# A RetNet block with its MLP: the second norm by halves of rows with its pieces further apart, one pair of operands tile by tile, and weight sums one POOL operation at a time

## The chip, the cores and the metric

The kernel runs on 1 core of one Trainium2 chip. A time is the device time of one execution in microseconds (us). The span of a profile runs from the first to the last instruction of the core. Three runs of the kernel before gave 1489.48, 1494.76 and 1496.14 us, so its time is the median, 1494.76 us. The profiled execution took 1489.55 us, and its span is 1487.8 us.

## What is computed

The depth is 1 and the mixer is retention, so the reference comes down to this (1024 tokens, 1024 features, 4 heads, an MLP of 4096):

```python
h = rmsnorm(x, norm_mix_pre)
q, k, v, g = split(h @ ret_w_in)            # 1024, 1024, 2048, 2048 columns
o = causal retention per head (decay gamma_h, head size 256 / 512)
o = head_norm(o, ret_gn) * silu(g)
x = x + rmsnorm(o @ ret_w_out, norm_mix_post)
h = rmsnorm(x, norm_mlp_pre)
h = square(relu(h @ mlp_w_up)) @ mlp_w_down
out = x + rmsnorm(h, norm_mlp_post)
```

## The kernel before

Every matmul with full precision is three: an operand is split into a high part (ACT copies it to fp32r) and a low part (DVE subtracts the copy from the source), and high x high, high x low and low x high are added up in PSUM. The gate, out, up and down matmuls are done in blocks of two by two with seven products in place of eight (`SEVEN`, L479), so sums of blocks are needed on both sides.

Work is laid down as a list of *units* in the order of TensorE's work. A unit's cost is its count of 512-column matmuls. Everything else hangs on that list: a `Job` names how many units of cost ahead of its use a load or a split is issued, a `background` entry (L516, L537) names a place in the first stage, and a piece of a norm stands in a `Chunks` list with a place of its own. An engine then runs its instructions strictly in the order in which they were laid down; SP issues all DMAs, also in order.

The stages are: (1) projections and retention by head, up to about 495 us, with the background: `weight_sums` loads 1 MB of w_out or w_down, POOL forms four sums of blocks (L509) and SP stores them, 24 times through one buffer (`sums_pool`); `feature_sums` does the same for the normed rows, 4 times, with four rebuilds (L526) and four sums (L531). Head norms (L407) and the causal masks (`affine_select`, L367, on POOL) run among them. (2) The gates, to about 665 us. (3) `down_stage("r")`, the out projection, L852: seven products m = 0 to 6 of 96 matmuls each, in steps of 24 whose operands are loaded 64 and split 34 units ahead (`Step`, L799; two staging buffers, three operand tiles in `acts3`). The last product is the one where the last `O_OUTER` = 2 steps are done together, output tile by output tile. (4) `Up`: `fill` (L686) runs the first two products of all 16 column pairs, 384 matmuls, with TensorE accumulating the second product into the bank that ACT has just copied to `k_u` (L641). It needs only rows 4 to 7 of the normed activations; the other five products (`rest`) need rows 0 to 3 too. (5) `down_stage("m")`, and the last norm, `fin`.

The second norm, `mix`, ties (3) to (4). It handles two rows of tiles at a time (u = 0, 1: rows 4 to 7; u = 2, 3: rows 0 to 3):
- `mix_a` (L979): ACT squares both rows of 1024 and takes the root; POOL multiplies both rows by the gain, four operations of 512 (L942).
- `mix_b` (L984): DVE makes 1/root with five small operations (`inverse`, L947), adds the row to the residual (L945); SP stores it; ACT squares the result.
- `mix_c` (L991): DVE again `inverse`, then the normed row (L994).
- `mix_first` (u < 2): TensorE transposes (L1004), ACT and DVE split. `mix_d`, `mix_e`, `mix_f` (u >= 2): transposes, then four sums of blocks, each split by ACT and DVE. `mix_f` ends with two DVE operations (L1052, L1053), the ACT copy of T4 (L1054) and its low part.

Places are counted from the start of product m = 5 (0); m = 6 ends at 192. Up to 192 a piece is laid down after the next 6 units; from then on `between` (L1113) calls `mix.place` only after every 24: at 216, 240, 264 and so on to 576. Of these stops 216, 264, 312, ... come after two first products (whose `k_u` copies stand just before), and 240, 288, 336, ... after two second ones. In the kernel before, `mix_a` of rows 0 and 1 has place 196, `mix_b` 218, `mix_c` 244, `mix_d` 262 and 302, `mix_e` 276 and 316, `mix_f` 288 and 328; rows 2 and 3 come 150 later.

## Time and profile before

| | before |
|---|---|
| median of 3 runs | 1494.76 us (1489.48 to 1496.14) |
| the profiled execution | 1489.55 us |
| its span | 1487.8 us |
| TensorE busy in it | 1435.7 us (96%) |
| VectorE (DVE), ScalarE (ACT), GpSimd (POOL) busy | 870.1, 567.4, 401.2 us |
| mean granted TensorE clock | 0.988 |

A page of the profile gives each engine's busy time. The view of waits names for one engine which instruction waited for which. The timeline lists instructions in order of time, merged; at the end of a line, in brackets, is the idle time before it and what ended it. The view of windows gives for a stretch of time the busy time of each engine and the clock that TensorE was granted (1.00 is 2.4 GHz, 0.50 is 1.2 GHz; a figure between them is a mean over the stretch).

### The profile page before, as it was taken

Reading aid. Unit: us, or ns where it says so; the run is one execution under the profiler, and the core shown is the slowest. Engines: PE = TensorE matmul, PEld = TensorE weight load, DVE = VectorE, ACT = ScalarE, POOL = GpSimd, SP = SyncE. Lnnn points to the kernel's source line nnn. Section 1 sums busy time; section 2 is a strip of 40 time slices with the busy share of each in tenths; the row PEclk is TensorE's granted clock in tenths of the full one; section 3 lists DMA queues with packets and bytes.
Section 4 is the critical chain, followed back from the end, with each engine's and each line's share of the span. In section 5 each row is a group of like instructions: output and inputs, shape, how many; then the busy total and the mean of one; then the engine's idle time right before and its main releaser. Section 6 shows DMA issues by size and latency. Waiting matters only on the chain.

```text
span 1487.8 us, 17555 instructions
## 1 busy us (share of the span) xinstructions
PE 1435.7 (96%) x6417; PEld 1179.5 (79%) x6417; DVE 870.1 (58%) x1194; ACT 567.4 (38%) x857; POOL 401.2 (27%) x344
## 2 busy tenths in 40 slices
PE   8999999999999999999998798999999999999996
PEld 6887888878888788788886676888888788888875
DVE  6446146356335468874448677588778553445556
ACT  6322222213222442234445455354454444343442
POOL 1213546254633003431002231234443300000212
PEclk9999999999999999999999999999999999999998
DMA  6316556455534697777565545576677755455654
GB/s 245 124 73 211 198 169 221 151 192 207 222 115 157 208 322 230 251 258 234 206 245 212 179 157 184 184 248 221 221 244 237 244 220 187 174 212 214 232 218 169
DMA packets 177623, 304.76 MB, mean 205 GB/s; under 512 B 11761, under 2 KB 85505, under 8 KB 177026
## 3 DMA queue, kind: packets, MB, share of 16 engines
q1 hardware_dynamic: 177394, 303.39, 58.9%
q8 instruction: 50, 0.82, 0.2%
q14 instruction: 35, 0.29, 0.1%
q10 hardware_dynamic: 144, 0.26, 0.0%
HBM read 207.14 MB, written 96.47 MB: 204 GB/s over the span
## 4 chain that ended last, share of the span: by engine, by line
PE 79%; DVE 7%; DMA 4%; issue 4%; ACT 4%; POOL 1%; SPq 0%; DVEq 0%; ACTq 0%; POOLq 0%
PE pXm L848 12%; PE pqk L299 12%; PE pv L324 11%; PE pXr L848 6%; PE pZu L565 5%; PE pVu L565 5%; PE pVg L565 3%; PE pYm L848 3%; PE pZg L565 3%; PE pYu L565 3%; PE pXu L565 2%; PE po L378 2%; DMA st_m<-in_mlp_w_down_dram 2%; PE pst L399 2%; PE pXg L565 2%
## 5 line engine op out<-in xcount | busy, mean ns | idle before, releaser
L841 DVE TENSOR_TENSOR o_m<-st_m,o_m 128x1024 fp32r<-128x1024 f32 (+1 forms) x84 | 135.3, 1639 | 143.1 <-ACT o_m L837 141.9
L509 POOL TENSOR_TENSOR wsum<-wsum 128x512 f32<-128x512 f32 x96 | 127.5, 1328 | 159.8 <-DMA wsum<-in_ret_w_out_dram 73.6
L837 ACT CAST o_m<-st_m 128x1024 fp32r<-128x1024 f32 (+1 forms) x84 | 110.6, 1338 | 134.9 <-DMA st_m<-wdt_T 51.9
L848 PE MATMUL pXm<-o_m 128*128 128x512 f32 x480 | 115.2, 394 | 4.0 <-DVE o_m L841 3.3
L848 PE MATMUL pXm<-o_m,o_m 128*128 128x512 f32 x480 | 113.0, 390 | 0.9 <-DVE o_m L841 0.9
L848 PE MATMUL pXr<-o_r 128*128 128x512 f32 x480 | 110.3, 390 | 1.7 <-DVE o_r L841 1.7
L848 PEld LDWEIGHTS pXm<-o_m 128*128 128x128 f32 x480 | 91.0, 190 | 24.6 <-DVE o_m L841 4.5
L848 PEld LDWEIGHTS pXr<-o_r 128*128 128x128 f32 x480 | 89.8, 188 | 20.6 <-DVE o_r L841 2.1
L848 PEld LDWEIGHTS pXm<-o_m,o_m 128*128 128x128 f32 x480 | 90.0, 188 | 20.1 <-DVE o_m L841 1.5
L841 DVE TENSOR_TENSOR o_r<-st_r,o_r 128x2048 fp32r<-128x2048 f32 x28 | 65.4, 2339 | 63.2 <-ACT o_r L837 63.0
L942 POOL TENSOR_TENSOR yd<-yd,gain 128x512 f32<-128x512 f32 x15 | 23.5, 1592 | 281.4 <-ACT junk L180 281.4
L324 PE MATMUL pv<-wv_0h,hT 128*128 128x512 f32 x256 | 86.7, 400 | 0.0
L324 PE MATMUL pv<-wv_1h,hT 128*128 128x512 f32 x256 | 86.0, 395 | 0.0
L1107 ACT ACTIVATE a<-c_u 128x512 f32<-128x512 f32 x48 | 30.4, 633 | 115.5 <-DVE c_u L665 100.8
L837 ACT CAST o_r<-st_r 128x2048 fp32r<-128x2048 f32 x28 | 53.5, 1910 | 50.8 <-DMA st_r<-wot_T 34.2
L331 DVE SCALAR_TENSOR_TENSOR v<-pv,dec,v 128x512 fp32r<-128x512 f32 x32 | 24.0, 750 | 73.8 <-ACT v L330 73.7
L307 ACT COPY qk<-pqk 128x512 f32<-128x512 f32 x32 | 18.8, 586 | 121.8 <-PE pqk L299 121.8
L942 POOL TENSOR_TENSOR y<-y,gains 128x512 f32<-128x512 f32 x16 | 22.6, 1442 | 158.1 <-DMA gains<-in_norm_mix_post_dram 99.1
L189 DVE TENSOR_TENSOR q<-pqk,q 128x512 fp32r<-128x512 f32 x16 | 11.0, 690 | 85.9 <-ACT q L188 85.9
L330 ACT ACTIVATE v<-pv,dec 128x512 fp32r<-128x512 f32 x32 | 22.0, 688 | 96.6 <-PE pv L324 93.0
L324 PEld LDWEIGHTS pv<-wv_1h,hT 128*128 128x128 f32 x256 | 48.7, 190 | 10.0
L324 PEld LDWEIGHTS pv<-wv_0h,hT 128*128 128x128 f32 x256 | 48.4, 189 | 9.8 <-ACT hT L188 0.2
(697 smaller groups left out, 3261.0 us busy)
## 6 DMA issues: line engine op xcount, KB each, us to landing
wsum<-in_mlp_w_down_dram SPq DMA_DIRECT2D x16, 1024.0 KB, 4.9
wdt_T<-wsum SPq DMA_DIRECT2D x64, 256.0 KB, 2.6
st_u<-in_mlp_w_up_dram SPq DMA_DIRECT2D x16, 1024.0 KB, 5.9
st_m<-m_S SPq DMA_DIRECT2D x32, 512.0 KB, 3.3
st_m<-wdt_T SPq DMA_DIRECT2D x32, 512.0 KB, 4.5
st_m<-m_A SPq DMA_DIRECT2D x24, 512.0 KB, 3.6
st_m<-in_mlp_w_down_dram SPq DMA_DIRECT2D x24, 512.0 KB, 4.5
wsum<-in_ret_w_out_dram SPq DMA_DIRECT2D x8, 1024.0 KB, 5.5
```

What stands on the lines that cost most here:

```text
L299: T.matmul(ps, hi_lo[a][:, k, :], hT[0][half, k // 4][:, b, k % 4, :], start=(k == 0 and i == 0), stop=(k == NK - 1 and i == 2))
L324: T.matmul(ps, hT[0][half, k // 4][:, a, k % 4, c * P:(c + 1) * P], w[b][:, k % 2, :], start=(k == 0 and i == 0), stop=(k == NK - 1 and i ...
L331: V.scalar_tensor_tensor(v[:, 1, :], ps, sc, f(v[:, 0, :]), op0=OP.mult, op1=OP.subtract)
L378: T.matmul(ps, q_parts[h, dt, half][:, a, c * P:(c + 1) * P], hi_lo[b][:, dt, :], start=(n == 0), stop=False)
L399: T.matmul(st_ps[h][dt], kt[h, t][:, a, dt * P:(dt + 1) * P], vt[h, t][:, b, :], start=(t == 0 and a == b == 0), stop=(keep and b == 1), s ...
L509: G.tensor_tensor(out_, x_, y_, op=OP.subtract)
L565: T.matmul(ps, w[:, x_, k * P:(k + 1) * P], b[:, y_, k, :], start=(first and k == i == 0), stop=(k == 3 and i == 2), skip_group_check=True)
L837: A.copy(hi, src(x_))
L841: V.tensor_tensor(lo, src(x_), f(hi), op=OP.subtract)
L848: T.matmul(banks[c], self.t[x_][:, q, c * P:(c + 1) * P], self.t[2 + y_][:, q, :], start=(start and q == i == 0), stop=(stop and q == 1 an ...
L942: eng.tensor_tensor(y[t][:, c], y[t][:, c], bc[g][:, c], op=OP.mult)
L1107: A.activation(a, c, AF.Relu)
```

## The change

- `weight_sums` and `feature_sums`: every POOL operation is an event of its own. The four sums of weights stand at 28, 37, 46, 55 behind the load in place of all at 28; the stores at 70 in place of 62. The rebuilds of features stand at 0, 8, 16, 24 and the sums at 34, 42, 50, 58, in place of 0 and 24; the stores at 70 in place of 60.
- `Step` in the out projection: loads and splits come 26 units earlier (90 and 60 ahead). The step j = 1 of each product has its operand in four single tiles of the pool `slots2` (15 tiles), no longer in `acts3`. `O_OUTER` is 1.
- `mix`: the half of a row that is ready first is squared and weighted early (`row_half`, for rows 4 to 7 during m = 4, for rows 0 to 3 during m = 6), the other half in `mix_a`; `row_root` adds the two sums with an ACT Identity whose bias is the other sum. The squares at the end of `mix_b` are a piece of their own (`mix_b2`), and so is the end of `mix_f` (`mix_g`). All places are listed in `START`. The gains are loaded at -88. `place` is called from m = 4 on.
- `fin` gets the same halves for rows 0 to 3, and its gain is loaded at -170.

```diff
         background.extend([(where, 0, load), (where, 70, store)])
+        background.extend([(where, 28 + 9 * n, lambda n=n: add(n)) for n in range(4)])
...
+        background.append((where, 70, store))
+        for n in range(4):
+            background.append((where, 8 * n, lambda n=n: rebuild(n // 2, n % 2)))
+            background.append((where, 34 + 8 * n, lambda n=n: add(n)))
...
-            self.job = Job((64 + more, self.load, "load"), (34 + more, self.split))
+            deep = 26 if name[0] == "r" else 0
+            self.job = Job((64 + more + deep, self.load, "load"), (34 + more + deep, self.split))
...
-                    if m >= 5:
+                    if m >= 4:
...
+    def row_half(ts, dh, g):
+        c = slice(dh * 512, (dh + 1) * 512)
+        for i, t in enumerate(ts):
+            if dh == 1:
+                sums[ts, i] = small.tile([P, 2], F32, name="s_halves", bufs=8)
+            squares(y[t][:, c], sums[ts, i][:, dh:dh + 1])
+            weighted(G, t, g, (dh,))
+
+    def row_root(ts):
+        ss = small.tile([P, len(ts)], F32, name="s_ss1")
+        for i, t in enumerate(ts):
+            p_ = sums.pop((ts, i))
+            A.activation(ss[:, i:i + 1], p_[:, 0:1], AF.Identity, bias=p_[:, 1:2])
+        s = small.tile([P, len(ts)], F32, name="s_root")
+        A.activation(s, ss, AF.Sqrt, scale=1.0 / D, bias=eps_col[:, 0:1])
+        rs[ts] = ss, s, len(ts)
+
     def mix_a(ts):
-        rs[ts] = sum_squares([y[t] for t in ts], "s_ss1")
-        for t in ts:
-            weighted(G, t, "mix_post")
+        row_half(ts, 0, "mix_post")
+        row_root(ts)
...
+    def mix_b2(ts):
         rs[ts] = sum_squares([xr[t] for t in ts], "s_ss2")
...
+    def mix_g(t, c):
         A.copy(view_u("T4", 0, c), part["t4"])
         low(V, "T4", c)
         part.clear()
 
-    mix.add(0, mix_begin)
-    for u in range(4):
+    mix.add(-88, mix_begin)
+    START = ((-70, 4, 18, 32, 44, 64), (-52, 70, 84, 98, 112, 134), (110, 188, 202, 216, 230, 250),
+             (122, 206, 326, 340, 354, 376))
+    for u, (a0, a1, b1, b2, c1, d1) in enumerate(START):
         ts = ORDER[2 * u:2 * u + 2]
-        a = 6 + 84 * u if u < 2 else 196 + 150 * (u - 2)
         for t in ts:
-            mix.add(a - 30, lambda t=t: load_row(t, x))
-        mix.add(a, lambda ts=ts: mix_a(ts))
-        mix.add(a + 22, lambda ts=ts: mix_b(ts))
-        mix.add(a + 48, lambda ts=ts: mix_c(ts))
+            mix.add(b1 - 50, lambda t=t: load_row(t, x))
+        mix.add(a0, lambda ts=ts: row_half(ts, 1, "mix_post"))
+        mix.add(a1, lambda ts=ts: mix_a(ts))
+        mix.add(b1, lambda ts=ts: mix_b(ts))
+        mix.add(b2, lambda ts=ts: mix_b2(ts))
+        mix.add(c1, lambda ts=ts: mix_c(ts))
...
-                mix.add(a + 66 + 8 * n, lambda t=t, c=c: mix_first(t, c), 2)
+                mix.add(d1 + 8 * n, lambda t=t, c=c: mix_first(t, c), 2)
...
-                mix.add(a + 66 + 40 * n, lambda t=t, c=c: mix_d(t, c), 2)
-                mix.add(a + 80 + 40 * n, lambda t=t, c=c: mix_e(t, c))
-                mix.add(a + 92 + 40 * n, lambda t=t, c=c: mix_f(t, c))
+                d = d1 + 44 * n
+                mix.add(d, lambda t=t, c=c: mix_d(t, c), 2)
+                mix.add(d + 12, lambda t=t, c=c: mix_e(t, c))
+                mix.add(d + 24, lambda t=t, c=c: mix_f(t, c))
+                mix.add(d + 34, lambda t=t, c=c: mix_g(t, c))
...
-    O_OUTER = 2
-    down_stage("r", r7, w_out, wo_t, NG, O_OUTER, y_mix, lambda j: False, mix.place)
+    O_OUTER = 1
+    down_stage("r", r7, w_out, wo_t, NG, O_OUTER, y_mix, lambda j: j == 1, mix.place)
...
-    fin.add(0, fin_begin)
+    fin.add(-170, fin_begin)
...
-            fin.add(a + 24, lambda c=c: fin_a((c - 1, c)))
-            fin.add(a + 50, lambda c=c: fin_b((c - 1, c)))
+            fin.add(-150 + 24 * c, lambda c=c: row_half((c - 1, c), 1, "mlp_post"))
+            fin.add(a, lambda c=c: fin_a((c - 1, c)))
+            fin.add(a + 20, lambda c=c: fin_b((c - 1, c)))
```

## Rows read from the trace of the kernel before

**Rows 1.** The page: busy time, share of the span and instructions of each engine

```profile
PE 1435.7 (96%) x6417; PEld 1179.5 (79%) x6417; DVE 870.1 (58%) x1194; ACT 567.4 (38%) x857; POOL 401.2 (27%) x344
```

**Rows 2.** Waits of TensorE: who waited for whom, us in total, times, longest

```profile
PE ptr L1004 <- DVE y L994: 12.4, 3, 6.4
PE pXu L565 <- ACT k_u L641: 10.1, 4, 3.7
...
PE po L378 <- DVE stl L189: 2.8, 1, 2.8
...
PE po L390 <- POOL sc L367: 2.2, 2, 2.0
```

**Rows 3.** Windows: PE, PEld, DVE, ACT, POOL busy (count), granted clock, DMA share, GB/s

```profile
774.50:946.00 171.50, 147.01 (x642) 119.67 (x641) 119.90 (x161) 86.29 (x146) 39.48 (x31) 0.94 0.57 192
...
840.00:860.00 20.00, 13.59 (x58) 11.21 (x58) 14.70 (x21) 9.30 (x19) 7.78 (x6) 0.83 0.56 184
...
320.00:335.00 15.00, 12.16 (x49) 9.42 (x48) 11.06 (x19) 2.99 (x7) 9.94 (x11) 0.89 0.49 155
```

**Rows 4.** Timeline of PE, 796 to 933: start, duration, instructions, [idle before, releaser]

```profile
796.26 1.94 PE L1004 MATMUL ptr<-ident,y 128*128 128x128 f32 x8 [5.29 <-DVE y L994]
...
825.10 1.04 PE L1004 MATMUL ptr<-ident,y 128*128 128x128 f32 x8
...
854.34 1.94 PE L1004 MATMUL ptr<-ident,y 128*128 128x128 f32 x8 [6.41 <-DVE y L994]
...
859.37 2.88 PE L565 MATMUL pXu<-uB,w_u3A 128*128 128x512 f32 x12
862.09 2.88 PE L565 MATMUL pXu<-uB,w_u4A 128*128 128x512 f32 x12
...
883.44 4.60 PE L565 MATMUL pXu<-uB,w_u6A 128*128 128x512 f32 x12 [2.56 <-ACT k_u L641]
...
898.98 3.06 PE L565 MATMUL pXu<-uB,w_u8A 128*128 128x512 f32 x12 [2.77 <-ACT k_u L641]
...
927.10 5.40 PE L565 MATMUL pXu<-uB,w_u12A 128*128 128x512 f32 x12 [3.66 <-ACT k_u L641]
```

**Rows 5.** Timeline of ACT, 882 to 897

```profile
882.28 0.62 ACT L1054 CAST uT<-t 128x512 fp32r<-128x512 f32 x1 [2.08 <-DVE t L1053]
882.81 1.07 ACT L641 COPY k_u<-pXu 128x512 f32<-128x512 f32 x2
...
895.78 1.06 ACT L180 ACTIVATE junk<-xr 128x1024 bf16<-128x1024 f32 x1 [4.33 <-DVE xr L945]
```

**Rows 6.** Timeline of POOL, 313 to 330 and 839 to 846

```profile
313.85 5.40 POOL L509 TENSOR_TENSOR wsum<-wsum 128x512 f32<-128x512 f32 x4 [6.14 <-issue]
...
324.20 5.33 POOL L531 TENSOR_TENSOR hs<-hs,hs 128x512 f32<-128x512 f32 x4
...
839.84 5.95 POOL L942 TENSOR_TENSOR y<-y,gains 128x512 f32<-128x512 f32 x4 [25.41 <-ACT junk L180]
```

**Rows 7.** Timeline of DVE: a small operation alone and beside POOL, and a normed row

```profile
93.28 0.16 DVE L174 SCALAR_TENSOR_TENSOR s_q<-s_t,s_r 128x1 f32<-128x1 f32 x1
...
320.55 1.22 DVE L174 SCALAR_TENSOR_TENSOR s_q<-s_t,s_r 128x1 f32<-128x1 f32 x1
...
852.91 2.48 DVE L994 SCALAR_TENSOR_TENSOR y<-xr,s_q,gains 128x1024 f32<-128x1024 f32 x2
```

**Rows 8.** Groups of ACT instructions by form: busy us, mean ns of one | idle before

```profile
L180 ACT ACTIVATE junk<-xr 128x1024 bf16<-128x1024 f32 x8 | 8.5, 1057 | 18.4 <-DVE xr L945 18.2
...
L180 ACT ACTIVATE junk<-yd 128x512 bf16<-128x512 f32 x8 | 5.0, 623 | 16.0 <-DVE yd L888 16.0
...
L167 ACT ACTIVATE s_sqrt<-s_var 128x1 f32<-128x1 f32 x32 | 6.5, 203 | 90.8 <-DVE s_var L414 90.8
```

**Rows 9.** Waits of the DMA queue on SP

```profile
SPq L503 <- DMA wdt_T<-wsum: 28.7, 20, 5.7
```

**Rows 10.** Timeline of PE in the gates' fill, 505 to 509

```profile
505.61 3.27 PE L565 MATMUL pXg<-hT,w_g2A 128*128 128x512 f32 x12 [0.47 <-ACT w_g2A L617]
```

More of the change, by code (lines that the diff above doesn't have):

```diff
@@ L503, in load, with add @@
             nc.sync.dma_start(t, w[p * 256:(p + 1) * 256, :].rearrange("(f p) c -> p f c", p=P))
-        def add():
+        def add(n):
             t = keep["t"]
             b11, b12, b21, b22 = (t[:, i, n * 512:(n + 1) * 512] for i in range(2) for n in range(2))
-            for out_, x_, y_ in ((b11, b12, b11), (b12, b22, b12), (b22, b22, b11), (b21, b21, b22)):
-                G.tensor_tensor(out_, x_, y_, op=OP.subtract)
+            out_, x_, y_ = ((b11, b12, b11), (b12, b22, b12), (b22, b22, b11), (b21, b21, b22))[n]
+            G.tensor_tensor(out_, x_, y_, op=OP.subtract)
         def store():
@@ L514, in store, with rebuild, add @@
                 nc.sync.dma_start(dst[n, p // 2][:, p % 2, :], t[:, i, j * 512:(j + 1) * 512])
-        background.extend([(where, 0, load), (where, 28, add), (where, 62, store)])
+        background.extend([(where, 0, load), (where, 70, store)])
+        background.extend([(where, 28 + 9 * n, lambda n=n: add(n)) for n in range(4)])
     def feature_sums(k, where):
         keep = {}
-        def rebuild():
-            for i in range(2):
-                for j in range(2):
-                    t = keep[i, j] = scratch(f"hs{i}{j}", [P, 512])
-                    b = hT[0][j, i]
-                    G.tensor_tensor(t, f(b[:, 0, k, :]), f(b[:, 1, k, :]), op=OP.add)
-        def add():
+        def rebuild(i, j):
+            t = keep[i, j] = scratch(f"hs{i}{j}", [P, 512])
+            b = hT[0][j, i]
+            G.tensor_tensor(t, f(b[:, 0, k, :]), f(b[:, 1, k, :]), op=OP.add)
+        def add(n):
             b11, b12, b21, b22 = keep[0, 0], keep[0, 1], keep[1, 0], keep[1, 1]
-            for out_, x_, y_ in ((b11, b12, b11), (b12, b22, b12), (b22, b22, b11), (b21, b21, b22)):
-                G.tensor_tensor(out_, x_, y_, op=OP.subtract)
+            out_, x_, y_ = ((b11, b12, b11), (b12, b22, b12), (b22, b22, b11), (b21, b21, b22))[n]
+            G.tensor_tensor(out_, x_, y_, op=OP.subtract)
         def store():
@@ L535, in store @@
                 nc.sync.dma_start(th[n][:, k, :], keep.pop(at))
-        background.extend([(where, 0, rebuild), (where, 24, add), (where, 60, store)])
+        background.append((where, 70, store))
+        for n in range(4):
+            background.append((where, 8 * n, lambda n=n: rebuild(n // 2, n % 2)))
+            background.append((where, 34 + 8 * n, lambda n=n: add(n)))
     for i in range(NG + NU):
@@ L1142, in fin_a @@
     def fin_a(ts):
-        rs[ts] = sum_squares([y[t] for t in ts], "s_ss1")
-        for t in ts:
-            weighted(G, t, "mlp_post")
+        row_half(ts, 0, "mlp_post")
+        row_root(ts)
     def fin_b(ts):
```

## The prediction, made before the changed kernel was run

> **What bounds the kernel now.** I read the page's busy times first: TensorE is busy 1435.7 of 1487.8 us [rows 1]. No other engine is near that, so only two things can shorten the kernel: time in which TensorE waits, and time in which it runs at the lower clock. The second view was therefore TensorE's waits. Four lines carry most of them: 12.4 us for normed rows (L994), 10.1 us for the ACT copy `k_u`, and 2.8 and 2.2 us in the retention stage, for a DVE split and a POOL mask [rows 2]. The third view, windows, places the first two. From the start of product m = 5 (774.5) to the first `rest` product (946) TensorE is busy 147.0 us of 171.5 at a mean granted clock of 0.94 [rows 3].
>
> What would this stretch take without waits? It holds 192 matmuls of the out projection (m = 5, 6) and 384 of `fill`. Twelve of them follow one another in 862.09 - 859.37 = 2.72 us [rows 4], so 576 take 130.6 us. The 64 transposes add 8 groups; a group lasts 1.04 us where twelve matmuls last 2.88 [rows 4] and free the engine 0.16 sooner, so 0.85 us each, 6.8 in all. Sum 137, against 171.5: **34 us** are lost here. 24.5 of them are idle (171.5 - 147.0). The other 10 are mostly the lower level of 1.2 GHz that follows a long wait: behind the wait of 3.66 us twelve matmuls have a duration of 5.40 instead of 2.88, behind that of 2.56 us 4.60; behind the wait of 2.77 only 3.06 [rows 4].
>
> The timelines say who is late. At 854.34 the transposes wait 6.41 us for a row that DVE finishes at 852.91 + 2.48 = 855.39, counted over both rows [rows 4, 7]: `mix_c` (244) and `mix_d` (262) fall on the same stop, 264, with no matmul between them. At 883.44 TensorE waits for `k_u`, which ACT starts at 882.81, directly behind L1054; that copy had itself waited 2.08 us for the last DVE sum of `mix_f` [rows 5]. The wait of 3.66 us at 927.10 has the same form. At 898.98 `k_u` stands behind the squares of `mix_b`, which waited 4.33 us for DVE [rows 4, 5]. At 796.26 the first rows wait 5.29 us [rows 4]. So the losses come from ACT's and DVE's strict order, not from their load.
>
> **The change, part by part.** *Second norm.* Work removed: none. Work added: squares in halves, 2 x 623 ns for 1057 ns and one more accumulator read [rows 8], some 0.4 us for each of 12 rows, and 12 Identity operations of 128x1. No row has Identity; the nearest is the 128x1 root with 203 ns [rows 8]. From 0.1 to 1.5 us each I take 0.2. Together 7 us of ACT over 700 us. They hide behind ACT's idle time (it is busy 567 of 1488 us [rows 1]); uncovered they would cost those 7 us. Work moved: half of POOL's multiplications. Four take 5.95 us [rows 6]; two are left on the path of each pair, so `mix_b` can start about 3 us sooner.
>
> Each wait goes as follows. Rows 4 and 5: `mix_a` at 4 to the transposes at 64 are 60 units, 13.6 us, for a chain of root (about 4 us with queueing), weighting and `mix_b` (4), squares and root (3) and `mix_c` (3.5, from two rows in 2.48 [rows 7] and five small operations): 14.5 less what overlaps, so 0 to 1 us of the 5.29 stays. Rows 6 and 7 have 64 units and no wait. Rows 0 and 1: `mix_c` moves to stop 240, `mix_d` stays at 264, and 24 matmuls (5.44 us) lie between, against 2.5 + 1: the 6.41 us go. `mix_e` now falls on 264 too, so at 288 `mix_f` finds its sums ready; `mix_g` still falls on 288 with it, and the wait of 2.08 us in ACT's order stays, but starts some 3 us earlier, ahead of the `k_u` that is due 5.4 us after the stop. At 336 the same, with about 0.6 us to spare. Rows 2 and 3: `mix_b` at 336 and `mix_b2` at 360 no longer share a stop, so the squares wait for nothing (2.77 gone). But `mix_b2` and `mix_c` both fall on 360 and the transposes on 384: `k_u` 0.9, squares and root 2.8, five small operations 0.9, one row 1.24 make 5.8 against 5.44, so 0.5 to 1 us of new wait. `mix_f` and `mix_g` of row 2 get different stops (408, 432), those of row 3 share 456, after the `k_u` pair; the 3.66 go.
>
> What is late next is the supply of `fill`: SP loads, ACT splits, DVE splits, two staging buffers. The gates' fill, which has no norm in it, waits 0.47 us once like that [rows 10] and about as much a second time, in 8 column pairs; for 16 at full speed I take 2 us, and 1.5 for one fall of the clock. Left over: 1 + 1 + 3.5, say 5 us. **Gain 29 us**, bounds 14 (rival a) and 34.
>
> *Out projection.* Loads and splits 26 units (5.9 us) earlier give the operands 13.6 in place of 7.7 us of room against a DVE that now waits inside `mix_b` and `mix_c` for 1 to 3 us. Each such wait holds the low parts queued behind it on DVE, and the next load on SP that needs their staging buffer. An `acts3` tile is free 72 units before its next use and a split asks for it 60 before, so it isn't waited for. The four single tiles of j = 1 live 84 of every 96 units; with four rows of y and up to four of x that is 12 of 15 tiles. Where the stage begins, the first split asks for a tile that the last gate's S2 product frees 12 units later: ACT stands 2.7 us, with the last two gate operands behind it, due 5.4 us after. I take 0; if that cover is gone it costs up to 3 us. *O_OUTER* and the early gains: 0, since nothing waits for them now that the split comes earlier.
>
> *POOL operations one at a time.* Twelve operations in a row kept POOL busy from 313.85 to 329.5 [rows 6]. Beside them a DVE operation on 128x1 took 1.22 us, alone 0.16 [rows 7]; several such held back the split that TensorE then missed for 2.8 us [rows 2]. With gaps of 9 units (2.04 us) between operations of 1.33, a mask waits behind one operation, not four, and DVE gets in between. Up to 5.0 us of waits and 1.6 of lower clock (0.89 over 15 us [rows 3]) can be gained. Against it: the stores move 8 units later and the next load stands 73.6 units after the one before, so 3.6 units (0.8 us) behind them instead of 11.6. SP already waits for these stores 20 times, 28.7 us in total [rows 9]; 24 waits grow by up to 1.8 us, and POOL's first sum, 6.3 us behind its load, with the masks queued behind it, by as much. Bounds: a loss of 3 and a gain of 6.6; I take a **gain of 4**.
>
> The trace shows a DVE operation of 0.16 us stretched to 1.22 beside POOL [rows 7]. The Trainium skill says why (SBUF — State Buffer, "Who interferes with whom"): a VectorE instruction with two SBUF inputs shares a read port with GpSimd, and the one issued second waits until the other ends. By that rule spreading takes away no blocked time and lets each POOL operation hit another DVE operation; that result is the last rival below.
>
> *Fin.* The same halves for rows 0 to 3, during m = 4 and 5 of the last projection, where TensorE doesn't wait for them: 0, bounds -1 and +1.
>
> Sum: 1489.55 - 29 - 4 = 1456.5 for an execution like the profiled one, whose span lies 1.75 us below its time. That one is 5.2 us below the median of the runs. Nothing in the rows says whether the changed kernel keeps this distance; I add 1.5 us: **1458 us**.
>
> **The rivals.** (a) *The stops eat the spacing.* Beyond 192 a piece moves only in steps of 24, so `mix_f` and `mix_g` stay together at 288 and 336, and SP and ACT supply `fill` late at full speed. For it: the gates' fill waits even now [rows 10]. Against it: ACT is idle half the time there (86.3 of 171.5 us [rows 3]). If the `k_u` waits (10.1 us and 5 of lower clock behind them) and 4 us of phase 1 stay, 1456.5 + 19 = **1475**. (b) *The waits move whole*: operands of the out projection wait for single tiles, or ACT for its tile at the stage's start, and hold back what the norm gains. For it: 12 of 15 tiles. Against it: only 4 more than before. 7 steps with 3 to 4 us each give back 25: about **1484 to 1492**. (c) *Slower, by the lock*: each of 24 chunk steps of the retention waits for one POOL operation more, 1.3 us, and falls to the lower clock, 1.5 us. All 24 would cost 67 and give **1527**; from 13 of them on (36 us) the kernel is slower by more than the bound. For it: 1.22 against 0.16 us. Against it: with runs of four only two such steps waited longer than 1 us.
>
> **How the numbers follow.** Forecast (1447 to 1468) 0.57; (a), 1468 to 1482, 0.25; (b) 0.11, most of it near no change; (c) 0.07. The range 1447 to 1480 leaves out some 0.2. A measurement of this kernel can tell about 0.5% (7.5 us) from no change: faster below 1487.3. That takes the forecast, (a) and a part of (b): 0.85; same 0.08; slower 0.07.
>
> **What would show it.** Right: between the start of m = 5 and the first `rest` product 137 to 145 us, a clock near 1.00 there, no wait of transposes for L994 above 1.5 us, and `k_u` no more behind a waiting L1054; in the retention no PE wait over 1 us. Wrong: `k_u` waits as before at 288 and 336 (a); waits of PE for `o_r`, or of ACT for a tile at the stage's start (b); more than ten PE waits for `sc` or `stl` in the first 495 us (c).

## The result, and the profile after

The changed kernel takes 1471.81 us, median of 4 runs (1471.24 to 1473.12); beside it the kernel before took 1493.15 us (4 runs, 1489.48 to 1496.14). The ratio is 0.986, 95% interval 0.983 to 0.989: faster, by 21 us (1.4%). The prediction said 1458.0 with a range of 1447 to 1480. The range holds the time; the point lies 13.8 us below it, so of the forecast gain of 36.8 us (1494.76 to 1458.0) some 60% came.

The page's first line, the waits of TensorE (who waited for whom: us in total, times, longest) and two windows of after (columns as in [rows 3]) answer to [rows 1 to 3]:

```profile
PE 1427.8 (97%) x6417; PEld 1172.9 (80%) x6417; DVE 872.4 (59%) x1201; ACT 571.9 (39%) x900; POOL 411.2 (28%) x344
...
PE ptr L1026 <- DVE y L1016: 8.8, 4, 6.3
PE pXu L567 <- ACT k_u L643: 3.0, 2, 1.9
PE pVg L567 <- DVE c_g L667: 2.9, 2, 2.5
PE pXr L851 <- ACT y L870: 2.4, 1, 2.4
...
PE po L378 <- DVE stl L189: 1.9, 1, 1.9
...
PE po L390 <- POOL sc L367: 1.3, 2, 1.1
...
776.83:931.22 154.39, 141.52 (x641) 115.67 (x640) 118.46 (x161) 84.00 (x162) 37.61 (x27) 0.98 0.59 198
...
814.00:820.00 6.00, 3.09 (x12) 2.83 (x13) 5.08 (x6) 1.17 (x2) 1.43 (x2) 0.50 0.49 188
```

The `k_u` waits fell from 10.1 to 3.0 us, those for a normed row from 12.4 to 8.8, and 6.34 of these 8.8 are one wait. Two lines ahead of the down projection are new: `c_g` in the gates and the copy of `y` in the out projection. From the start of m = 5 to the first `rest` product the kernel takes 154.39 us in place of 171.50 [rows 3].

Cut at the same products, the two profiled spans compare like this (us; the two columns on the right are the kernels of experiments 2 and 11):

| stretch | before | after | late halves | wider |
|---|---|---|---|---|
| start to the gates' fill | 494.10 | 491.12 | 490.85 | 493.04 |
| the gates' fill | 49.45 | 49.00 | 49.12 | 49.57 |
| rest of the gates | 122.03 | **125.14** | 125.25 | 122.21 |
| out projection, m = 0 to 4 | 108.92 | **111.58** | 111.68 | 109.25 |
| out projection, m = 5 and 6 | 56.95 | 55.87 | **47.83** | 48.03 |
| `fill` of the up projection | 114.49 | **98.52** | 98.47 | **92.41** |
| `rest` | 217.60 | 217.60 | 217.60 | 217.60 |
| down projection, m = 0 to 4 | 219.74 | 219.71 | 219.72 | 219.73 |
| down projection, m = 5 and 6 | 93.20 | **89.77** | 90.54 | 88.71 |
| last product to the end | 11.32 | 11.69 | 11.66 | 11.31 |
| span | 1487.81 | 1469.99 | 1462.72 | 1451.87 |

So `fill` gave 16 us, but m = 5 and 6 almost nothing (1.1); two stretches that the prediction left at 0 grew by 3.1 and 2.7 us; one that it left at 0, the last two products of the down projection, shrank by 3.4.

**The wait of 6.34 us.** It is the transposes of row 6. Timelines of after: TensorE, DVE and POOL (start, duration, instruction; in brackets the idle time before and its releaser):

```profile
816.91 1.94 PE L1026 MATMUL ptr<-ident,y 128*128 128x128 f32 x8 [6.34 <-DVE y L1016]
...
806.11 4.53 DVE L844 TENSOR_TENSOR o_r<-st_r,o_r 128x2048 fp32r<-128x2048 f32 x2
810.56 1.23 DVE L953 TENSOR_SCALAR s_ms<-s_ss 128x2 f32<-128x2 f32 x1
811.70 0.15 DVE L955 RECIPROCAL s_r<-s_root 128x2 f32<-128x2 f32 x1
811.89 1.11 DVE L957 TENSOR_TENSOR s_t<-s_r 128x2 f32<-128x2 f32 x1
813.04 1.18 DVE L958 SCALAR_TENSOR_TENSOR s_t<-s_t,s_ms 128x2 f32<-128x2 f32 x1
814.25 1.19 DVE L960 SCALAR_TENSOR_TENSOR s_q<-s_t,s_r 128x2 f32<-128x2 f32 x1
815.48 2.48 DVE L1016 SCALAR_TENSOR_TENSOR y<-xr,s_q,gains 128x1024 f32<-128x1024 f32 x2
...
809.01 6.41 POOL L945 TENSOR_TENSOR y<-y,gains 128x512 f32<-128x512 f32 x4 [10.81 <-ACT junk L180]
```

DVE makes 1/root for rows 6 and 7 just while POOL does the new early multiplications of rows 0 to 3 (places 110 and 122; `mix_c` of rows 6 and 7 has 112). Four of five small operations take 1.1 to 1.2 us, together 4.71, where four of [rows 7]'s 0.16 would be 0.64: 4.1 us. The row itself is not slower, and POOL's four operations take 6.41 in place of 5.95 us [rows 6]. Two low parts of `o_r` (4.53 us) stand ahead of the small operations on DVE. The granted clock is 0.50 from 814 to 820 (the window above): that is the last 2.9 us of the wait and 3.1 us of matmuls behind it, among them the eight transposes that take 1.94 us.

**The two new waits.** Timelines of after, ACT and TensorE, at the end of the gates and in m = 0:

```profile
649.11 0.62 ACT L619 CAST w_g7A<-st_g 128x512 fp32r<-128x512 f32 x1
656.12 1.91 ACT L840 CAST o_r<-st_r 128x2048 fp32r<-128x2048 f32 x1 [6.40 <-DMA st_r<-in_ret_w_out_dram]
657.94 0.61 ACT L619 CAST w_g7S<-s_g7S 128x512 fp32r<-128x512 f32 x1
661.06 0.63 ACT L776 ACTIVATE sg<-c_g 128x512 f32<-128x512 f32 x1 [2.51 <-DVE c_g L667]
...
689.95 1.90 ACT L840 CAST o_r<-st_r 128x2048 fp32r<-128x2048 f32 x1 [3.81 <-DMA st_r<-wot_T]
691.75 1.06 ACT L870 COPY y<-pXr 128x512 f32<-128x512 f32 x2
...
661.11 3.08 PE L567 MATMUL pVg<-hT,w_g7S 128*128 128x512 f32 x12 [2.50 <-DVE c_g L667]
...
692.38 2.79 PE L851 MATMUL pXr<-o_r 128*128 128x512 f32 x11 [2.37 <-ACT y L870]
```

The cast of the out projection's first operand now stands 26 units earlier in ACT's order, but its load (issued by SP at 649.46) has not landed: ACT stands for 6.40 us, with the gates' last operand `w_g7S` behind it, DVE's `c_g` behind the low part that follows, and TensorE behind that. In m = 0 the same cast stands ahead of the copies that free the bank.

Why is the load late, though it too was moved by 26 units (5.9 us)? SP's issue of it and SP's own waits in after, summed over the whole execution:

```profile
649.46 1.12 SPq L821 DMA_DIRECT2D st_r<-in_ret_w_out_dram  x1
...
SPq L814 <- DVE o_r L844: 82.6, 24, 7.8
...
SPq L766 <- ACT sg L776: 38.5, 13, 6.6
```

At the end of the gates SP had stood 6.6 us, up to 643.90, for ACT's `sg`, and issued other transfers before it came to this load. Counted from the first product of the rest of the gates the load goes out 109.3 us behind it (649.46 - 540.12), and with the old places (experiment 3) 110.4 (652.11 - 541.73): about 1 us earlier, not 5.9. In m = 0 SP issues the load in question at 683.06, having waited 1.8 us for DVE's low part of an earlier `o_r` to free one of the two staging buffers (L814).

### The profile page after: what moved, and what is told of

Same layout as the page of the kernel before. It is cut to its first block, busy times and chain, and to the rows that moved or that the text cites. A ratio compares the mean times of both kernels' runs of the same rounds, so it can differ in the third digit from the quotient of the medians.

```text
span 1470.0 us, 17597 instructions
## 1 busy us (share of the span) xinstructions
PE 1427.8 (97%) x6417; PEld 1172.9 (80%) x6417; DVE 872.4 (59%) x1201; ACT 571.9 (39%) x900; POOL 411.2 (28%) x344
## 4 chain that ended last, share of the span: by engine, by line
PE 72%; DVE 8%; DMA 8%; ACT 4%; issue 4%; POOL 3%; SPq 0%; DVEq 0%; ACTq 0%; POOLq 0%
PE pXm L851 11%; PE pv L324 9%; PE pqk L299 9%; PE pZu L567 5%; PE pVu L567 5%; PE pXr L851 5%; PE pXu L567 3%; PE pYm L851 3%; PE pYu L567 3%; PE pZg L567 3%; PE pVg L567 3%; PE po L378 2%; DMA st_m<-in_mlp_w_down_dram 2%; POOL wsum L509 2%; PE pXg L567 2%
## 5 line engine op out<-in xcount | busy, mean ns | idle before, releaser
L844 DVE TENSOR_TENSOR o_m<-st_m,o_m 128x1024 fp32r<-128x1024 f32 (+1 forms) x84 | 139.4, 1691 | 136.7 <-ACT o_m L840 136.3
L509 POOL TENSOR_TENSOR wsum<-wsum 128x512 f32<-128x512 f32 x96 | 131.0, 1365 | 183.9 <-DMA wsum<-in_mlp_w_down_dram 89.1
L945 POOL TENSOR_TENSOR yd<-yd,gain 128x512 f32<-128x512 f32 x15 | 28.6, 1923 | 273.2 <-ACT junk L180 273.2
L844 DVE TENSOR_TENSOR o_r<-st_r,o_r 128x2048 fp32r<-128x2048 f32 (+1 forms) x35 | 69.4, 2006 | 57.5 <-ACT o_r L840 57.5
L851 PE MATMUL pXr<-o_r 128*128 128x512 f32 x360 | 83.4, 390 | 2.4 <-ACT y L870 2.4
L851 PEld LDWEIGHTS pXr<-o_r 128*128 128x128 f32 x360 | 67.4, 188 | 16.7 <-ACT y L870 2.8
L840 ACT CAST o_r<-st_r 128x2048 fp32r<-128x2048 f32 (+1 forms) x35 | 54.4, 1567 | 54.5 <-DMA st_r<-wot_T 24.4
L725 POOL TENSOR_TENSOR t_u<-a_u,q_u 128x512 f32<-128x512 f32 x16 | 20.7, 1291 | 129.5 <-issue 99.6
```

The costliest lines, as they stand in the source:

```text
L509: G.tensor_tensor(out_, x_, y_, op=OP.subtract)
L840: A.copy(hi, src(x_))
L844: V.tensor_tensor(lo, src(x_), f(hi), op=OP.subtract)
L851: T.matmul(banks[c], self.t[x_][:, q, c * P:(c + 1) * P], self.t[2 + y_][:, q, :], start=(start and q == i == 0), stop=(stop and q == 1 an ...
L945: eng.tensor_tensor(y[t][:, c], y[t][:, c], bc[g][:, c], op=OP.mult)
```

## The experiments

Each ratio is to the kernel before, run on the same chip. The kernel before had medians of 1492.95 (experiments 1 to 4), 1492.15 (5 to 8) and 1493.31 us (9 to 12); these groups ran on three different chips, so a difference of 1 us between medians of different groups says nothing.

**1. The sums alone.** The kernel before with `weight_sums` and `feature_sums` of the changed one.

```diff
-        background.extend([(where, 0, load), (where, 28, add), (where, 62, store)])
+        background.extend([(where, 0, load), (where, 70, store)])
+        background.extend([(where, 28 + 9 * n, lambda n=n: add(n)) for n in range(4)])
```

> The kernel before with only the sums of weights and features laid down one POOL operation at a time. Theory: this part is worth about 3 us, all of it in the retention; the gates then start near 491 us (494.1 before, 491.1 in the changed kernel), the rest is as before: ratio to before 0.998. Rival (the lock): each POOL operation holds up another small DVE operation; more than ten TensorE waits for sc or stl in the first 495 us and a ratio above 1.000.

Measured: 1494.51 us (10 runs), ratio 1.001 (0.9997 to 1.0024). No gain. Its profiled execution was 2.4 us shorter up to the gates' fill, and 2.3 and 2.9 us longer in m = 5, 6 and `fill`.

**2. The early halves of rows 0 to 3 later.**

```diff
-    START = (..., (110, 188, 202, 216, 230, 250),
-             (122, 206, 326, 340, 354, 376))
+    START = (..., (146, 188, 202, 216, 230, 250),
+             (158, 206, 326, 340, 354, 376))
```

> The changed kernel with the early halves of rows 0 to 3 (POOL's four multiplications) at places 146 and 158 in place of 110 and 122, behind the normed rows 6 and 7. Theory (lock): those four POOL operations stretch the five small DVE operations of mix_c from 0.8 to 4.9 us and make TensorE wait 6.3 us for row 6; moved away, that wait falls to about 2 us, the clock doesn't fall, and the kernel takes 4 to 6 us less, 1466 to 1468 us. Rival (order): the two low parts that DVE does ahead of mix_c are the cause; the wait stays above 5 us, 1472 us.

Measured: 1467.49 us, ratio 0.983 (0.981 to 0.986). The wait for row 6 is gone, m = 5 and 6 take 47.83 us. That is more than the stretched operations explain: the edit also put the second low part of `o_r` behind the normed row in DVE's order (one of 2.28 us ahead of it, not two of 4.53 together). The profiled execution is the shortest of the four, 1464.43 us; between the medians the gain over the changed kernel is 4.3 us, not 8.

**3. Loads and splits of the out projection as before.**

```diff
-            deep = 26 if name[0] == "r" else 0
+            deep = 0
```

> The changed kernel with loads and splits of the out projection 64 and 34 units ahead again (deep = 0); tiles, O_OUTER and norm as changed. Theory: the early split makes ACT wait for a load at the head of its order, which costs 2.5 us at the last gate product and 2.4 us at the end of product m = 0; without it the two stages are some 5.8 us shorter and the kernel takes about 1466 us. Rival: the room is needed in m = 5 and 6; then waits of TensorE for o_r appear there and eat the gain, 1470 to 1478 us.

Measured: 1466.50 us, ratio 0.982 (0.980 to 0.984). Both new waits are gone: rest of the gates 122.26, m = 0 to 4 108.93 us. Over all profiled executions the two stretches together take 236.7 to 237.4 us in six kernels with the earlier loads and 230.9 to 231.5 in seven without (232.1 in an eighth, experiment 7). The early loads cost about 5.8 us there, 5.3 between the medians. The rival's fear for m = 5 and 6 shows only in small waits, 1.09 us for row 4 (0.30 in after) and 0.74 us for an `o_r`; the stretch takes 55.60 us, in after 55.87.

**4. The last norm as before.**

```diff
-    fin.add(-170, fin_begin)
+    fin.add(0, fin_begin)
...
-            fin.add(-150 + 24 * c, lambda c=c: row_half((c - 1, c), 1, "mlp_post"))
-            fin.add(a, lambda c=c: fin_a((c - 1, c)))
-            fin.add(a + 20, lambda c=c: fin_b((c - 1, c)))
+            fin.add(a + 24, lambda c=c: fin_a((c - 1, c)))
+            fin.add(a + 50, lambda c=c: fin_b((c - 1, c)))
```

> The changed kernel with the last norm of rows 0 to 3 as before (whole rows, places 72 to 170, gain loaded at 0). Theory: its later stores of the output hold up SP's operand loads behind them; the last two products take 93.2 us again in place of 89.8 and the kernel 3 us more, 1475 us. Rival: the 3.4 us are chance of one execution; 1472 us.

Measured: 1477.98 us, ratio 0.990 (0.988 to 0.992), 6.2 us more than the changed kernel, where the theory said 3. Of these m = 5 and 6 of the down projection make 4.5: 94.24 us in place of 89.77. The rest lies mostly in the gates and the out projection, which the edit does not touch. SP's waits from 1405 to 1443, of this kernel and then of after:

```profile
SPq L1180 <- DVE xr L948: 9.9, 2, 9.1
```

```profile
SPq L1179 <- DVE xr L948: 6.5, 2, 5.7
```

The store of the finished rows (L1180, in after L1179) waits in SP's order for DVE, with the operand loads behind it. In after it is issued 37.4 us behind the start of m = 5 (1405.89 - 1368.53) and the loads behind it catch up; with the old places it is issued 44.6 us behind (1415.18 - 1370.58), and TensorE then waits 0.98 and 1.83 us for operands at 1439 to 1442. That the later store causes these waits is read from the two timelines; no run moves the store alone. The edit to the last norm is worth about 4.5 us: nine profiled executions with it take 88.1 to 91.5 us there, five without 93.2 to 95.3.

**5. POOL's multiplications moved, ACT's squares not.**

```diff
+            if not (late and dh == 1):
+                weighted(G, t, g, (dh,))
...
+        if u > 1:
+            mix.add(a0 + 36, lambda ts=ts: [weighted(G, t, "mix_post", (1,)) for t in ts])
```

> Of rows 0 to 3 the squares of the first half stay at 110 and 122, as in the changed kernel; only POOL's multiplications of that half move by 36 units (8.2 us), to 146 and 158. The run with squares and multiplications moved together lost the wait of 6.34 us for row 6, but both engines had moved. Theory (POOL stretches DVE's small operations): the wait for row 6 goes here too, m = 5 and 6 of the out projection take 48 to 50 us in place of 55.87, total 1465 to 1468. Rival (ACT's four squares, ahead of the root of rows 6 and 7, make it late): the wait stays at 4 us or more, 54 to 56 us, total 1470 to 1473.

Measured: 1472.32 us, ratio 0.987 (0.984 to 0.989), the wait is 6.31 us. This looks like the rival, but POOL's timeline says that the run tells nothing apart:

```profile
810.62 6.41 POOL L945 TENSOR_TENSOR y<-y,gains 128x512 f32<-128x512 f32 x4 [10.80 <-ACT junk L180]
```

POOL had nothing in between, so it ran as soon as ACT's squares were done, 36 units of place notwithstanding: 32.2 us behind the start of m = 5 (778.44), in after 32.2 too (809.01 - 776.83). A place gives an order within an engine, not a time.

**6. Stops after every 12 matmuls in the fill.**

```diff
-            for _ in zip(a.first(), b.first()):
+            for _ in zip(a.first(), mid(between), b.first()):
...
-        fill_at[0] += 24
+        fill_at[0] += 12
...
-    START = (..., (110, 188, 202, 216, 230, 250),
-             (122, 206, 326, 340, 354, 376))
+    START = (..., (110, 188, 204, 216, 240, 264),
+             (122, 206, 336, 348, 360, 384))
```

> The changed kernel with stops in the fill after every 12 matmuls in place of 24, and the pieces of rows 0 to 3 put on stops of their own (second squares, normed rows, transposes, sums, ends: 12 or 24 apart). Theory (what is left in the fill are pieces that share a stop): the waits of 1.11 and 1.90 us for k_u and of 0.92 and 1.24 for a normed row go, with the lower clock behind them; the fill takes 92 to 95 us in place of 98.5, total 1465 to 1468. Rival (the fill is limited by the supply of its operands, loads and splits): the waits turn up at w_u operands, the fill stays at 97 or more, total 1470 to 1473. The out projection should not change (its wait for row 6 stays).

Measured: 1472.74 us, ratio 0.988 (0.985 to 0.990): no gain. `fill` takes 96.78 us. The waits of 1.11, 1.24 and 1.90 us went, the 0.92 stayed, and one for `k_u` of 2.51 us came. ACT's timeline of this kernel:

```profile
879.69 1.06 ACT L180 ACTIVATE junk<-xr 128x1024 bf16<-128x1024 f32 x1 [1.48 <-DVE xr L953]
...
882.27 0.56 ACT L643 COPY k_u<-pXu 128x512 f32<-128x512 f32 x1
```

I had put the squares of rows 2 and 3 on stop 348, between two `k_u` copies; they waited for DVE, and the second copy behind them. Not the supply: no wait for an operand is above 0.2 us in this `fill`. Experiment 11 puts the squares elsewhere.

**7. The second norm alone**, in the kernel before (halves, places, `mix_b2`, `mix_g`, `place` from m = 4).

```diff
-                    if m >= 5:
+                    if m >= 4:
...
+        row_half(ts, 0, "mix_post")
+        row_root(ts)
```

> The kernel before with the second norm of the changed one alone (halves, places, begin of the gains, place called from m = 4); weight sums, operands of the out projection, O_OUTER and the last norm as before. Theory (the norm's spacing carries the gain): fill 98 to 99 us in place of 114.5; the wait for row 6 appears here too (m = 5 and 6: 54 to 57 us); all other stages as before; total 1474 to 1479, a ratio of 0.988 to 0.991. Rival (the norm pieces need the operands tile by tile or the early loads): waits for o_r in m = 4 to 6, those products 60 us or more, total 1482 or more.

Measured: 1480.63 us, ratio 0.992 (0.990 to 0.994), between the two theories. `fill` takes 98.52 us as expected, but m = 5 and 6 take 63.15, with a wait of 11.10 us for row 6. ACT and DVE ahead of it:

```profile
812.48 1.90 ACT L837 CAST o_r<-st_r 128x2048 fp32r<-128x2048 f32 x1 [4.72 <-DMA st_r<-in_ret_w_out_dram]
...
814.41 2.29 DVE L841 TENSOR_TENSOR o_r<-st_r,o_r 128x2048 fp32r<-128x2048 f32 x1 [4.59 <-ACT o_r L837]
816.62 1.23 DVE L950 TENSOR_SCALAR s_ms<-s_ss 128x2 f32<-128x2 f32 x1
```

The last step's operand comes late, ACT and DVE stand for it in their order, and only then come the small operations, again beside POOL.

**8. Late halves, old loads and finer stops together** (the edits of experiments 2, 3 and 6).

> The changed kernel with three edits at once: first halves of rows 0 to 3 at 146 and 158, loads and splits of the out projection 64 and 34 units ahead as before, stops in the fill after every 12. Theory (each edit takes away a loss of its own): gates 122.3, out projection to m = 4 108.9, m = 5 and 6 48, fill 92 to 95, the other stages as in the changed kernel: total 1453 to 1458. Rival (the gains overlap, since the normed rows wait for the same DVE and a wait removed lets the next one through): 1460 to 1466, with waits of PE in m = 5, 6 or in the fill above 2 us.

Measured: 1457.81 us, ratio 0.977 (0.975 to 0.979), within the first theory. The gains add up: in the profiled executions, against after, 5.4 us in the rest of the gates and m = 0 to 4, 6.3 in m = 5 and 6 (49.62 us), 3.1 in `fill`, which takes 95.41 us with the `k_u` wait of experiment 6 (2.53 us); 14.0 between the medians.

**9. POOL really later.** The squares stay at 110 and 122; POOL multiplies both halves of rows 0 to 3 in `mix_a`, where it waits for later squares. DVE's order is unchanged.

```diff
+            if not late:
+                weighted(G, t, g, (dh,))
+            elif dh == 0:
+                weighted(G, t, g)
```

> In the changed kernel, ACT squares the first half of rows 0 to 3 at 110 and 122 as before, but POOL multiplies both halves only in the piece mix_a (188 and 206), behind ACT's later squares; so POOL really runs later, and the order of DVE's instructions is that of the changed kernel. Theory (POOL stretches DVE's small operations): those four take 0.16 us in place of 1.1 to 1.2, the wait of 6.34 us for row 6 falls by 4 us to 2.0 to 2.6, m = 5 and 6 take 50 to 53 us in place of 55.87; total 1466 to 1470. What then stays of the wait is the second low part of o_r that stands ahead of the small operations. Rival (the order of DVE's and ACT's queues alone makes row 6 late): the wait stays above 5.5 us, m = 5 and 6 at 55 to 57. POOL's four multiplications in a row at 188 may cost up to 2 us in the fill in either case.

Measured: 1468.85 us, ratio 0.984 (0.982 to 0.987); m = 5 and 6 take 50.10 us. Timelines of this kernel, DVE and TensorE:

```profile
807.59 4.52 DVE L844 TENSOR_TENSOR o_r<-st_r,o_r 128x2048 fp32r<-128x2048 f32 x2
812.03 0.16 DVE L953 TENSOR_SCALAR s_ms<-s_ss 128x2 f32<-128x2 f32 x1
...
812.68 0.16 DVE L960 SCALAR_TENSOR_TENSOR s_q<-s_t,s_r 128x2 f32<-128x2 f32 x1
...
814.31 1.06 PE L1029 MATMUL ptr<-ident,y 128*128 128x128 f32 x8 [2.24 <-DVE y L1019]
```

All five small operations are back at 0.16 us and the wait falls from 6.34 to 2.24, by the 4.1 us worked out above. That settles the cause of these 4.1 us: POOL's multiplications. The 2.24 us that stay match the second low part of `o_r`, 2.2 us, which experiment 2 had moved away. The median is 3.0 us below that of the changed kernel, but the two intervals overlap (0.982 to 0.987 and 0.983 to 0.989), so the proof is the trace and not the total.

**10. The second norm with `O_OUTER` = 1** (experiment 7 and one line).

```diff
-    O_OUTER = 2
+    O_OUTER = 1
```

> The kernel before with the second norm of the changed one, and O_OUTER = 1 in place of 2; operands, loads, sums and last norm as before. With the norm alone, m = 5 and 6 took 63.15 us, with a wait of 11.10 us for row 6: ACT stood 4.72 us before the cast of an operand whose load had come late, DVE 4.59 us behind it, and then the stretched small operations. Theory (the last two steps done together make the loads late, so O_OUTER = 1 mends that): the wait falls to 6 to 7 us, m = 5 and 6 to 55 to 58 us, total 1472 to 1476. Rival (it is the operand tile by tile that mends it): the wait stays above 9 us, 61 us or more, total 1478 to 1483.

Measured: 1474.27 us, ratio 0.989 (0.986 to 0.991). The wait is 4.32 us (the stretched small operations are still there), m = 5 and 6 take 56.12. So this line, put at 0 in the prediction, is worth 6.4 us between the medians (7.0 in this stretch) once the norm stands in m = 6: the cast that had waited 4.72 us for its load no longer stands ahead of row 6. The operand tile by tile is not needed for it. Both kernels have the loads and splits at their old places; no run has `O_OUTER` = 2 with the early ones.

**11. Wider.** The kernel of experiment 8 with

```diff
-    START = ((-70, 4, 18, 32, 44, 64), ..., (146, 188, 204, 216, 240, 264),
-             (158, 206, 336, 348, 360, 384))
+    START = ((-70, 4, 18, 32, 44, 70), ..., (146, 188, 204, 216, 240, 276),
+             (158, 206, 348, 372, 396, 420))
```

> The kernel with all three edits (late halves, loads of the out projection as before, stops after every 12), and pieces still further apart: transposes of rows 4 and 5 at 70 in place of 64, of rows 0 and 1 at 276 in place of 264, the pieces of rows 2 and 3 from mix_b on 12 to 36 later, the second squares at 372, where no k_u copy is due. Theory (what is left are pieces too near to each other): the waits of 2.53 us for k_u and of 1.10 and 0.92 for normed rows go, total 1451 to 1455. Rival (something else is as late: other waits of 1 to 2.5 us come up in the fill, or rest waits for the last sums): 1456 to 1460.

Measured: 1453.25 us (1452.47 to 1454.09), ratio 0.974 (0.972 to 0.976). Window of this kernel from m = 5 to `rest`, and its longest wait in `fill`:

```profile
774.06:914.51 140.45, 138.47 (x642) 114.58 (x640) 113.95 (x163) 87.09 (x164) 37.30 (x27) 1.00 0.68 227
...
PE pXu L567 <- DVE w_u8A L622: 1.4, 1, 1.4
```

The clock stands at 1.00 and 2 us of idle time are left. No wait for a normed row or `k_u` of 0.5 us or more stays: what had been left in `fill` were pieces too near to each other, and its supply costs no more than this 1.4.

**12. Wider, with the old sums** (runs of four POOL operations as one event; stores at 62 for the weights and 60 for the features).

> The same kernel with the weight sums of the kernel before (four POOL operations as one event, store at 62); the feature sums stay one at a time. Theory (the spread sums are worth what the prediction said): 3 to 5 us slower than the run beside it, all of it in the stretch up to the gates' fill, with waits of about 2 us for sc and 2.8 for stl. Rival (the difference of the retention is no more than the spread of executions): within 2 us of the run beside it, in either direction.

The edit puts back the sums of features too, which the expectation says it leaves; so the run judges both kinds of sums together.

Measured: 1450.82 us (1450.48 to 1455.67), ratio 0.973 (0.970 to 0.975). It can't be told from the run beside it, experiment 11. Up to the gates' fill its profiled execution took 490.13 us, the other 493.04. Taken over all, four executions with the old sums took 490.1 to 494.1 us there (mean 492.5), ten with the new ones 490.9 to 493.6 (mean 491.9).

Both kernels are faster than the changed one, by 19 and 21 us.

## Why the prediction was right or wrong

**The sum.** Between the two profiled executions the span fell by 17.8 us, where 33 were forecast: 17.1 in the second norm's stretch (forecast 29), 3.4 up to the end of the gates' fill (forecast 4), a loss of 5.8 in the rest of the gates and m = 0 to 4 (forecast 0), and 3.1 behind `rest` (forecast 0). That the range holds the time is in part luck: the last norm brought a gain that the prediction had not counted. Without it (experiment 4) the kernel took 1477.98 us, 2 us inside the end of the range at 1480.

**The signs of being right** were mostly missed: 154.39 us in place of 137 to 145 from m = 5 to `rest`, a clock of 0.98 there, one wait for a normed row of 6.34 us where none was to pass 1.5, in the retention still 1.92 us for `stl` and 1.1 for `sc`, and at stop 336 `k_u` still stood behind a cast that waited.

**What bounds the kernel**: right. All gains and losses are TensorE's waits and the clock behind them; `rest` and m = 0 to 4 of the down projection, without waits, stayed within 0.1 us in all profiled executions.

**Second norm, gain 29, measured 17.** The mechanism was right, three terms were not.
- "Rows 6 and 7 have 64 units and no wait": wrong, and the dearest step. Row 6 waited 6.34 us; without POOL's early multiplications it is 2.24, and with the second low part moved too it is nothing. From 55.87 to 47.83 us that is 8 us in the profiled executions, 4.3 between the medians. The prediction had the price in its rows (1.22 beside POOL, 0.16 alone [rows 7]) and used it for the retention stage only. It counted the five operations of `mix_c` at 0.9 us and did not look at which POOL work the change itself puts beside them: 110 and 122 against 112.
- Rows 4 and 5, 0 to 1 us left of the 5.29: right (0.30; 1.09 with the loads as before).
- Rows 0 and 1 and `k_u` at stops 288 and 336: the 6.41 became 0.92, and at 288 there is no wait for `k_u`, as said. At 336, "about 0.6 us to spare", TensorE waited 1.11 us (2.56 before): ACT had waited 3.10 us for DVE's last sum of row 1 ahead of it.
- Rows 2 and 3, 0.5 to 1 us at stop 384: 1.24. Stop 432, "different stops, the 3.66 go": 1.90 stayed, for T4 of row 2 and the transposes of row 3 share that stop, and the casts of row 3 stand ahead of `k_u`. The timeline of ACT in after:

```profile
898.78 0.62 ACT L1078 CAST uT<-t 128x512 fp32r<-128x512 f32 x1 [2.77 <-DVE t L1075]
...
902.71 0.62 ACT L1066 CAST uT<-t 128x512 fp32r<-128x512 f32 x1 [0.18 <-DVE t L1057]
903.23 1.07 ACT L643 COPY k_u<-pXu 128x512 f32<-128x512 f32 x2
```

- Supply of `fill`, 3.5 us: too much. Its waits for operands are 0.39 and 0.67 us in after. The 98.52 us of `fill` are 6.1 above experiment 11, and these are the shared stops. The 142 us that the prediction gave the stretch can be had (140.45 there), with other places.

**Out projection, 0, at most 3 if the cover is gone**: wrong by 5.8 us. The bound named ACT's stand at the stage's start, but for a free tile, 2.7 us; it stood for a load, 6.40 us, and once more in m = 0. A split issued 26 units earlier needs a load that lands as much earlier. This one went out only about 1 us earlier, behind SP's wait of 6.6 us for ACT, and in m = 0 it waited for one of two staging buffers. With the loads as before the room was nearly sufficient (waits of 0.74 and 1.09 us in m = 5 and 6, experiment 3). The single tiles of j = 1 show nothing: `fill` and m = 5 and 6 take the same within 0.6 us with them (experiment 3) and without (experiment 10; the two differ besides in the sums and the last norm).

***O_OUTER*, 0**: not tested as it stands. The reason given was that "nothing waits for them now that the split comes earlier". With the split at its old place the term is worth 6.4 us, to the good, once `mix_c` stands in m = 6 (experiments 7 and 10). Whether the early split alone would have made it 0 stays open.

**POOL operations one at a time, 4**: not seen in the time (experiments 1 and 12). Why is in POOL's timeline of after, which answers to [rows 6]:

```profile
312.02 4.05 POOL L509 TENSOR_TENSOR wsum<-wsum 128x512 f32<-128x512 f32 x3 [6.12 <-issue]
316.03 1.28 POOL L525 TENSOR_TENSOR hs<-hT 128x512 f32<-128x512 f32 x1
317.27 1.28 POOL L509 TENSOR_TENSOR wsum<-wsum 128x512 f32<-128x512 f32 x1
318.51 3.78 POOL L525 TENSOR_TENSOR hs<-hT 128x512 f32<-128x512 f32 x3
322.25 1.28 POOL L530 TENSOR_TENSOR hs<-hs,hs 128x512 f32<-128x512 f32 x1
```

The operations are shuffled, but POOL, having stood for 6.12 us (the profile does not show for what), still runs nine of them without a gap, from 312.02 to 323.5; DVE's small operations beside them take up to 1.21 us as before, and the wait for `stl` is 1.92 in place of 2.82 [rows 2]. Spacing in the order list is no spacing in time for an engine that has a backlog.

**Fin, 0, bounds -1 and +1**: wrong by about 4.5 us, to the good (experiment 4). The prediction looked at TensorE's waits beside the moved pieces and not at SP, whose store waits for them with the loads of m = 6 behind it.

**The rivals.** (a) has the number (1468 to 1482 holds 1471.8), but not the mechanism that was priced: of the 15 us for `k_u` and the clock behind it at most 6 stayed in `fill` (98.52 against 92.41); the rest of the shortfall is the wait for row 6 and the loads. (b), operands that wait for tiles, did not show as such; the two new waits are its kin, at 5.8 us. (c), the slower case, had the right price in the wrong place: TensorE's waits for `stl` and `sc` in the retention did not grow (1.9 and 1.3 us, before 2.8 and 2.2 [rows 2]), but one `mix_c` got slower. Two sums of the rivals don't come out: the 25 us of (b) on top of 1458 give 1483, not 1484 to 1492; and from 1458, without the gain of 4, it takes 15 chunk steps of (c), not 13, to pass the bound of slower.

**The rule on the port.** In after, no RECIPROCAL was stretched (L955: 10 times, mean 156 ns, longest 166), not even the one at 811.70 amid POOL's run, while SCALAR_TENSOR_TENSOR of the same 128x2 was (L960: 10 times, mean 347 ns, one of them 1.19 us, in that run, and one 1.00). Groups of DVE instructions of after, by form:

```profile
L960 DVE SCALAR_TENSOR_TENSOR s_q<-s_t,s_r 128x2 f32<-128x2 f32 x10 | 3.5, 347 | 0.3
...
L955 DVE RECIPROCAL s_r<-s_root 128x2 f32<-128x2 f32 x10 | 1.6, 156 | 0.7 <-ACT s_root L997 0.7
```

That is what the Trainium skill says (SBUF — State Buffer, "Who interferes with whom"): a VectorE instruction with two SBUF inputs contends with a GpSimd instruction that reads SBUF; one with at most one such input, outside the modes that use two ports, does not. The page also counts `tensor_scalar` among those that may take the shared ports, and L953 agrees (1.23 us beside POOL, 0.15 alone).

## What to carry to other kernels

A piece that is moved out of the way lands beside something else: list, for each engine that it uses, what runs at its new place, and price small DVE operations beside a run of POOL operations at up to one POOL operation each (here four of five were hit). An earlier place helps only as far as the load behind it can be earlier too; otherwise the waiting instruction blocks its engine. And places give order, not time, so look at the moved engine's timeline before you believe an experiment that moves work.

## What the runs showed of the hardware that was not expected

Beside a run of POOL operations of 128x512, four DVE operations on 128x2 each took 1.1 to 1.2 us in place of 0.16, somewhat less than one of the POOL operations (1.6 us, 6.41 for four), so the chain of five took 4.9 us (810.56 to 815.48) instead of 0.85 (812.03 to 812.88 in experiment 9), while POOL's four took only 0.46 us more (6.41 against 5.95).

In a wait of TensorE of 6.34 us the granted clock fell to 0.50, and it stayed there for some 3.5 us behind it; a wait of 2.24 us left it at 1.00 (the next group of eight transposes lasted 1.06 us, after the long wait 1.94). The length of the wait alone does not decide: behind 2.51 us in experiment 6 the clock was 0.50 and twelve matmuls lasted 4.61 us, behind 2.53 us in experiment 8 it was 1.00 and they lasted 3.04.
